# Six weight staging buffers and earlier loads of layer 1's vectors in a two-layer hybrid diffusion kernel

## The chip, the cores and the metric

The kernel runs on one core of one Trainium2 chip. The metric is the device time of one execution in microseconds (us), given as the median of several runs. Lower is better.

## What is computed

Two layers act on 256 latent tokens `x` and 256 context tokens, each of width 1024. Each layer modulates a normed input with vectors made from `c` (for the latent) and `c_ctx` (for the context), projects it once, and feeds three mixers: latent attention over all keys (MLA), windowed attention with sinks (SWA), and a gated delta rule in chunks of 64, run in both directions. Their outputs are gated, summed and projected; a gated MLP with a depthwise convolution follows.

```python
for l in range(DEPTH):                       # DEPTH = 2
    m_lat = modulation(c, w_mod[l], b_mod[l])        # silu(c) @ w_mod + b_mod, split in 6
    m_ctx = modulation(c_ctx, w_mod[l], b_mod[l])
    xn = adaln(x, norm1[l], m_lat[0], m_lat[1])
    hn = adaln(h, norm1[l], m_ctx[0], m_ctx[1])
    y_lat, y_ctx = token_mixer(xn, hn, ...)          # MLA + SWA + gated delta, merge, w_out
    x = x + m_lat[2] * y_lat
    x = x + m_lat[5] * conv_ffn(adaln(x, norm2[l], m_lat[3], m_lat[4]), ffn_up[l], ffn_conv[l], ffn_down[l])
    ...                                              # h likewise, except in the last layer
return rmsnorm(x, norm_f)
```

All tensors are float32. The kernel keeps that precision by splitting each operand in a rounded high part and a low rest and multiplying three times.

## The kernel before

All tokens lie side by side, 512 columns, features on the partitions. A weight piece of 512 KB (four blocks of 128 input rows by 256 output columns) goes through `load_split` (L181 to L190): SyncE (SP) starts its DMA into a buffer of tag `raw`, ScalarE (ACT) casts it to `wh` (L189), VectorE (DVE) makes the rest `wl` (L179, called from L190), and TensorE (PE) multiplies each block three times in `mm3` (L199 to L201). There are `nr` = 3 buffers `raw`, `nh` = 3 of `wh` and `nl` = 4 of `wl`. A `raw` buffer is free again when its `wl` has been made.

The modulation vectors need 1024 x 6144 weights per layer. For layer 0, `mod_part` (L583 to L605) loads them in pieces of 128 x 1024 into the same `raw` buffers (L591), without casting them, and PE multiplies each piece as it stands (L593). Two generators of this work, `mods[0]` and `mods[1]`, fill gaps of layer 0: the first the scan of the delta rule (`gdn_scan`, from L923), the second the attentions. A `raw` buffer of theirs is free when PE has multiplied it.

The small vectors of a layer (biases, norms, the rows of a convolution) are loaded as rows of one tile by `load_vectors` (L538 to L559): nine DMAs, then two transposes on PE (L558) and two copies on DVE (L559). `load_conv` (L561 to L572) does the same for the 132 rows of an MLP convolution: two DMAs (128 rows at L567, 4 rows at L568), two transposes (L570, L571) and one copy. Layer 0's vectors load through GpSimd (POOL) at the start; layer 1's vectors and both convolutions load through SP at the start of layer 0's attentions (L1465 to L1468), all into buffers of tag `b2`, of which there are seven.

The order on each engine comes from a list scheduler of the framework: it takes instructions by priority as their inputs become ready in its own model. Each engine then works strictly in that order, and so does SP with its DMAs: a load whose buffer isn't free holds up every load behind it. DMAs on SP also wait for earlier ones, because their completion semaphores are reused in turn.

```python
        raw = self.sb(shape, "raw", F32, self.NRAW)
        for view, src in srcs:
            nc.sync.dma_start(out=view(raw), in_=src)
        H = self.sb(shape, "wh", F32R, self.NWH)
        L = self.sb(shape, "wl", F32R, self.NWL)
        nc.scalar.copy(H, raw)
        self.split_L(L, raw, H)
```

Of the kernel before, what the change touches and what calls it, by code (L numbers as in the profile page):

```python
# [5 lines left out]
F32 = mybir.dt.float32  # L6
# [12 lines left out]
DEPTH = 2  # L19
# [10 lines left out]
def make_consts():  # L30
# [58 lines left out]
    l1={}, s2=(2, 1, 2, 0), pe=(0.0, 0.1, 0.0, 0.0), ov=0, np=(0.1, 0.0, 0.25, 0), ly=2, qs=(0, 4), dec1=3.0, dec2=4.0, sol1=4.2, sol2=4.0,  # L89
    sol3=1.0, sol4=2.0, sca=(1.0, 2.0), scb=(1.0, 2.0), scc=(1.0, 2.0),   cap=12.0, sl=(0.3, 0.3, 0.5, 0.1), modc=(4.0, 0.9),  # L90
    lag=(0, 0, 2, 4, 5), nmod=(2, 5), hk=(5, 12), f0=(1.0, 1.6, 1.0, 1.0, 1.5, 1.0, 1.0), f1=(1.0, 1.0, 1.0, 0.3, 1.0, 1.0, 0.3), lat=1.0,
    bx=4, wd=0, dc=1, gk=(0, 0), hpe=60, w_t=5, w_k=3, w_s=0, w_r=1.5, w_n=3, w_o=4.0, nr=3, nh=3, nl=4, nb2=7, st=0, ab=(0.0, 0.0, 0.0, 0.0),
    st2=6, bge=2, hpa=40, hpn=0, hpk=40, hpv=40)

_INS = ["x", "c", "ctx", "c_ctx", "w_mod", "b_mod", "norm1", "norm2", "w_in", "mla_q_norm", "mla_kv_norm",
# [5 lines left out]
NVEC = 114  # L101
# [33 lines left out]
class Kernel:  # L135
# [402 lines left out]
    def load_vectors(self, l):  # L538

        nc, i = self.nc, self.ins  # L540
        q = nc.gpsimd if l == 0 else nc.sync
        ident = self.con("ident")
        rows = self.b2([128, 128])
        for nm, (r0, n) in VEC_ROWS.items():
            if nm == "gdn_norm":
                for h in range(2):
                    q.dma_start(out=rows[r0:r0 + 1, h * 64:h * 64 + 64], in_=i[nm][l:l + 1, :])
                continue
            a = i[nm] if nm == "norm_f" else i[nm][l]
            if nm == "gdn_conv":  # L550
                a = a.rearrange("t (r c) -> (t r) c", c=128)
            else:
                a = a.rearrange("(r c) -> r c", c=128)
            q.dma_start(out=rows[r0:r0 + n, :], in_=a)
        for a, b in ((0, 56), (56, NVEC)):
            yield
            ps = self.ps([128, T], "g")
            nc.tensor.transpose(ps[:, :b], rows[:b, :], ident[:b, :b])  # L558
            nc.vector.tensor_copy(self.vec[l][:, a:b], ps[:, a:b])  # L559

    def load_conv(self, l):  # L561

        nc, i = self.nc, self.ins
        ident = self.con("ident")
        fr = i["ffn_conv"][l].rearrange("t (r c) -> (t r) c", c=128)
        f0, f1 = self.b2([128, 128]), self.b2([128, 128])
        nc.sync.dma_start(out=f0, in_=fr[0:128, :])  # L567
        nc.sync.dma_start(out=f1[:4, :], in_=fr[128:132, :])  # L568
        ps = self.ps([128, T], "g")
        nc.tensor.transpose(ps[:, :128], f0, ident)  # L570
        nc.tensor.transpose(ps[:, 128:132], f1[:4, :], ident[:4, :4])  # L571
        nc.vector.tensor_copy(self.fcv[l], ps[:, :132])  # L572

    def v(self, l, nm):
        o, n = VEC_ROWS[nm]
# [721 lines left out]
    def layer(self, l):  # L1297
        nc, i = self.nc, self.ins
# [5 lines left out]
        n = self.qw = S if last else T  # L1304
# [77 lines left out]
        def push(*gens):  # L1382
            self.gsync()
            at = self.queue.index(self.gates) if self.gates in self.queue else len(self.queue)
            self.queue[at:at] = gens
# [5 lines left out]
        def chain(*gens, f=1.0, burst=0.0):  # L1391

            gens, value = list(gens), None
            while gens:
                for g in list(gens):
                    try:
                        self.fill(f * next(g), burst)
                    except StopIteration as e:
                        gens.remove(g)
                        value = e.value  # L1400
            return value
# [15 lines left out]
        spill = self.dram.tile([128, KD, T], F32, name=f"spill{l}")  # L1417
        for j in range(2):
            nc.sync.dma_start(out=spill[:, j * 4:j * 4 + 4], in_=self.xT[j])
        self.mark(f"gtab_{l}")  # L1420
        chain(self.gdn_tables(l), f=P[f"f{l}"][5])
        self.mark(f"gdec_{l}_0")
# [33 lines left out]
        if last:  # L1456
            t = self.s8([128, 8, n])
# [3 lines left out]
        nh = 8 // len(qh)  # L1461
        snk = self.sm([128, 8])
        nc.sync.dma_start(out=snk, in_=i["swa_sink"][l].partition_broadcast(128))
        if l == 0:
            for _ in self.load_vectors(1):  # L1465
                pass
            for j in range(DEPTH):
                self.load_conv(j)  # L1468
        push(*([gsp, mods[1]] if l == 0 else [gsp]))
        self.modcost = self.P["modc"][1]  # L1470
        ga = self.attend(streams, lambda h: ((qh[h // nh][:, h % nh, :], kh[h // 4][:, h % 4, :]),),
# [47 lines left out]
        for bi, ((gi, b), y) in enumerate(zip(gate_br, (yc, ya, yb))):  # L1519
# [4 lines left out]
            for u in range(4):  # L1524
                gate_load(bi * 4 + u + 2)
                if bi * 4 + u in ahead:
                    t = ahead.pop(bi * 4 + u)
# [61 lines left out]
        for half in range(2):  # L1589
            aH, aL = [], []  # L1590
            for a in (aH, aL):
                for al, m_ in ((self.s8, 4), (self.s8, 4), (self.b4, 2), (self.b4, 1)):
                    t = al([128, m_, T], F32R)
                    a += [t[:, k] for k in range(m_)]
            f0 = half * 11
# [124 lines left out]
```

## Time and profile before

| | before |
|---|---|
| median of 3 runs | 1764.64 us (1761.48 to 1771.3) |
| profiled execution | 1760.08 us, its span 1758.3 us |
| busy in the span: PE, DVE, ACT, POOL | 1668.4, 1160.7, 777.4, 217.0 us |
| mean granted TensorE clock | 0.976 of full speed |
| DMA traffic | 228.75 MB, mean 130 GB/s |

The busy time is a sum over stages with different limits; a stretch in which PE is idle is read with the engine and line that ended the idle time. The span is the profiled stretch; 1.8 us of the execution lie outside it.

### The profile page before, as it was taken

How to read it: one execution, taken by the hardware profiler on the slowest of the kernel's cores; microseconds unless marked ns; L12 is line 12 of the kernel's file. 1: busy time of each engine (PE TensorE's matmuls, PEld its weight loads, DVE VectorE, ACT ScalarE, POOL GpSimd, SP SyncE). 2: the span in 40 equal slices, each digit the busy share in tenths (PEclk: the TensorE clock that was granted, in tenths of full speed). 3: DMA queues.
4: the chain of work that ended last, by engine and by line, in shares of the span. 5: the costliest groups of instructions: out<-in, count | busy, mean ns of one | idle time of the engine just before them, and what ended most of it. 6: DMA issues, size and time to landing. Idle time of an engine off the chain costs nothing. (4 is left out here: it accounts for less than half of the span.)

```text
span 1758.3 us, 31525 instructions
## 1 busy us (share of the span) xinstructions
PE 1668.4 (95%) x12723; PEld 1355.3 (77%) x12723; DVE 1160.7 (66%) x2223; ACT 777.4 (44%) x1377; POOL 217.0 (12%) x217
## 2 busy tenths in 40 slices
PE   6989998998999999999999999989988899999997
PEld 3768766775557888668888888778887667999997
DVE  3888697675775534545435553699997877667684
ACT  3664412234665233324324433465532575556463
POOL 1000000002100312011001111020302301212010
PEclk9999998998999999999999999999897999999999
DMA  9424335333135533853233343434351223745663
GB/s 348 118 59 122 103 100 172 74 87 101 55 102 175 185 124 105 313 186 101 87 105 96 96 157 109 126 90 132 103 130 38 61 85 107 235 145 178 185 186 123
DMA packets 216944, 228.75 MB, mean 130 GB/s; under 512 B 51228, under 2 KB 195422, under 8 KB 215646
## 3 DMA queue, kind: packets, MB, share of 16 engines
q1 hardware_dynamic: 211582, 220.11, 40.9%
q10 hardware_dynamic: 4928, 6.56, 1.0%
q8 instruction: 100, 1.64, 0.4%
q14 instruction: 46, 0.38, 0.1%
q0 software_dynamic: 288, 0.06, 0.0%
HBM read 213.85 MB, written 11.80 MB: 128 GB/s over the span
## 5 line engine op out<-in xcount | busy, mean ns | idle before, releaser
L179 DVE TENSOR_TENSOR wl<-raw,wh 128x1024 fp32r<-128x1024 f32 (+2 forms) x294 | 357.7, 1217 | 236.9 <-ACT wh L189 235.7
L189 ACT CAST wh<-raw 128x1024 fp32r<-128x1024 f32 (+2 forms) x294 | 298.6, 1018 | 382.3 <-PE mm L200 187.6
L199 PE MATMUL mm<-xnh,wh 128*128 128x512 f32 (+2 forms) x1072 | 378.6, 354 | 4.6 <-DVE s L131 1.9
L201 PE MATMUL mm<-xnh,wl 128*128 128x512 f32 (+2 forms) x1072 | 373.2, 351 | 5.0 <-DVE wl L179 4.9
L200 PE MATMUL mm<-xnl,wh 128*128 128x512 f32 (+2 forms) x1072 | 374.4, 350 | 0.0
L199 PEld LDWEIGHTS mm<-xnh,wh 128*128 128x128 f32 (+1 forms) x1072 | 204.8, 191 | 39.2 <-issue 7.7
L201 PEld LDWEIGHTS mm<-xnh,wl 128*128 128x128 f32 (+1 forms) x1072 | 204.3, 191 | 35.6 <-DVE wl L179 7.0
L200 PEld LDWEIGHTS mm<-xnl,wh 128*128 128x128 f32 (+1 forms) x1072 | 204.8, 191 | 27.6 <-issue 4.0
L199 PE MATMUL g<-xnh,wh 128*128 128x256 f32 (+1 forms) x496 | 167.6, 340 | 1.4 <-ACT xnh L405 1.4
L200 PE MATMUL g<-xnl,wh 128*128 128x256 f32 (+1 forms) x496 | 166.3, 337 | 0.2 <-DVE xnl L406 0.2
L201 PE MATMUL g<-xnh,wl 128*128 128x256 f32 (+1 forms) x496 | 166.3, 337 | 0.0
L199 PE MATMUL mm<-s,wh 128*128 128x256 f32 (+1 forms) x458 | 149.4, 328 | 0.7 <-DVE s L534 0.6
L201 PE MATMUL mm<-s,wl 128*128 128x256 f32 (+1 forms) x458 | 149.3, 327 | 0.6 <-DVE wl L179 0.6
L200 PE MATMUL mm<-s,wh 128*128 128x256 f32 (+1 forms) x458 | 149.1, 326 | 0.1
L1620 POOL TENSOR_TENSOR b<-b,b 128x512 f32<-128x512 f32 (+1 forms) x44 | 54.4, 1237 | 442.1 <-DVE b L1604 381.1
L199 PEld LDWEIGHTS g<-xnh,wh 128*128 128x128 f32 x496 | 94.7, 192 | 15.0 <-issue 3.3
L201 PEld LDWEIGHTS g<-xnh,wl 128*128 128x128 f32 x496 | 94.7, 191 | 10.5 <-issue 1.2
L199 PE MATMUL g<-s,wh 128*128 128x512 f32 (+1 forms) x304 | 102.7, 338 | 0.0
L200 PEld LDWEIGHTS g<-xnl,wh 128*128 128x128 f32 x496 | 94.7, 191 | 10.1 <-DVE xnl L406 0.8
L200 PE MATMUL g<-s,wh 128*128 128x512 f32 (+1 forms) x304 | 102.2, 336 | 0.0
L201 PE MATMUL g<-s,wl 128*128 128x512 f32 (+1 forms) x304 | 102.1, 336 | 0.0
L199 PEld LDWEIGHTS mm<-s,wh 128*128 128x128 f32 x458 | 86.8, 190 | 8.8 <-DVE s L534 1.1
(290 smaller groups left out, 2699.0 us busy)
## 6 DMA issues: line engine op xcount, KB each, us to landing
raw<-in_w_in_dram SPq DMA_DIRECT2D x92, 512.0 KB
raw<-in_ffn_up_dram SPq DMA_DIRECT2D x80, 512.0 KB
s<-in_w_mod_dram SPq DMA_DIRECT2D x64, 512.0 KB
raw<-in_w_mod_dram SPq DMA_DIRECT2D x32, 512.0 KB
raw<-in_ffn_down_dram SPq DMA_DIRECT2D x32, 512.0 KB
raw<-in_w_out_dram SPq DMA_DIRECT2D x16, 512.0 KB
raw<-in_ffn_down_dram SPq DMA_DIRECT2D x16, 384.0 KB
spill<-s SPq DMA_DIRECT2D x4, 1024.0 KB
```

The lines of the kernel that those rows point to most:

```text
L179: self.nc.vector.tensor_tensor(out=out, in0=x, in1=h.bitcast(F32), op=ALU.subtract)
L189: nc.scalar.copy(H, raw)
L199: mm(ps, lhsT=wH, rhs=xH, start=start, stop=False)
L200: mm(ps, lhsT=wH, rhs=xL, start=False, stop=False)
L201: mm(ps, lhsT=wL, rhs=xH, start=False, stop=stop)
L1620: nc.gpsimd.tensor_tensor(out=y[:, cs], in0=y[:, cs], in1=av[t][:, cs], op=ALU.mult)
```

## The change

Six buffers `raw` stand in place of three; the room for them comes from a smaller scratch area for the descriptors that POOL writes for its own DMAs (2048 bytes in place of the default). `load_vectors(1)` and `load_conv` are split at a `yield`: their DMAs are issued right after layer 0's spill of the residual stream, ahead of the delta rule's tables, into three buffers of a new tag `rows`; transposes and copies stay at the start of layer 0's attentions. The four last rows of each convolution go into the vectors' tile, and the second transpose of each convolution takes that whole tile (122 rows). Each convolution is copied in two pieces.

```diff
-    bx=4, wd=0, dc=1, ... w_o=4.0, nr=3, nh=3, nl=4, nb2=7, ...
+    bx=4, wd=0, dc=1, ... w_o=4.0, nr=6, nh=3, nl=4, nb2=7, ...
@@ load_vectors
-        rows = self.b2([128, 128])
+        rows = self.b2([128, 128]) if l == 0 else self.sb([128, 128], "rows", F32, 3)
+        if l:
+            self.rows = rows
+            for j in range(DEPTH):
+                q.dma_start(out=rows[NVEC + 4 * j:NVEC + 4 * j + 4, :], in_=i["ffn_conv"][j].rearrange("t (r c) -> (t r) c", c=128)[128:132, :])
@@ load_conv
-        f0, f1 = self.b2([128, 128]), self.b2([128, 128])
+        f0, n = self.sb([128, 128], "rows", F32, 3), NVEC + 4 * DEPTH
         nc.sync.dma_start(out=f0, in_=fr[0:128, :])
-        nc.sync.dma_start(out=f1[:4, :], in_=fr[128:132, :])
+        yield
         ps = self.ps([128, T], "g")
         nc.tensor.transpose(ps[:, :128], f0, ident)
-        nc.tensor.transpose(ps[:, 128:132], f1[:4, :], ident[:4, :4])
-        nc.vector.tensor_copy(self.fcv[l], ps[:, :132])
+        nc.tensor.transpose(ps[:, 128:128 + n], self.rows[:n, :], ident[:n, :n])
+        nc.vector.tensor_copy(self.fcv[l][:, :128], ps[:, :128])
+        nc.vector.tensor_copy(self.fcv[l][:, 128:132], ps[:, 128 + NVEC + 4 * l:132 + NVEC + 4 * l])
@@ layer, after the spill
+        if l == 0:
+            small = [self.load_vectors(1)] + [self.load_conv(j) for j in range(DEPTH)]
+            for g in small:
+                next(g)
@@ layer, at the start of the attentions
         if l == 0:
-            for _ in self.load_vectors(1):
-                pass
-            for j in range(DEPTH):
-                self.load_conv(j)
+            for g in small:
+                for _ in g:
+                    pass
@@ kernel
-    nc = bacc.Bacc("TRN2", target_bir_lowering=False, num_devices=1)
+    nc = bacc.Bacc("TRN2", target_bir_lowering=False, num_devices=1, dynamic_dma_scratch_size=2048)
```

Three places show how the instructions move. Lines in the changed file are 4 to 9 higher from the edits on: L554 becomes L558, L558 becomes L562, L591 and L593 become L596 and L598, L1051 becomes L1056, L1233 becomes L1238, L1419 becomes L1424.

SP, the loads queued ahead of layer 0's attentions, before (`raw` from `in_w_mod` are the pieces of `mods[1]`; `b_599`, `b_602`, `b_603` hold the vectors and convolution rows):

```order
L591 DMA raw_4487<-in_w_mod_dram 128x1024
L591 DMA raw_4493<-in_w_mod_dram 128x1024
L1463 DMA sm_4092<-in_swa_sink_dram 128x8
L591 DMA raw_4559<-in_w_mod_dram 128x1024
L591 DMA raw_4565<-in_w_mod_dram 128x1024
L554 DMA b_599_4094<-in_b_mod_dram 48x128
...
L567 DMA b_602_4110<-in_ffn_conv_dram 128x128
L568 DMA b_603_4111<-in_ffn_conv_dram 4x128
...
L591 DMA raw_4617<-in_w_mod_dram 128x1024
L591 DMA raw_4623<-in_w_mod_dram 128x1024
```

and in the change:

```order
L596 DMA raw_4487<-in_w_mod_dram 128x1024
L596 DMA raw_4493<-in_w_mod_dram 128x1024
L596 DMA raw_4559<-in_w_mod_dram 128x1024
L596 DMA raw_4565<-in_w_mod_dram 128x1024
L596 DMA raw_4617<-in_w_mod_dram 128x1024
L1472 DMA sm_4108<-in_swa_sink_dram 128x8
L596 DMA raw_4623<-in_w_mod_dram 128x1024
L596 DMA raw_4689<-in_w_mod_dram 128x1024
```

The thirteen small loads are gone from this place, and the modulation pieces follow each other.

PE at the same place, before (`g_4051` is the rotary product of MLA's queries, `mm_4486` the modulation, `g_4104` to `g_4122` the transposes, `g_4126` and `g_4135` the first scores of the attention):

```order
L593 MATMUL mm_4486<-raw_4487,cT 32x256 x4
L593 MATMUL mm_4486<-raw_4493,cT 32x256
L1233 MATMUL g_4077<-b_593_4075,cst 128x256
L593 MATMUL mm_4486<-raw_4493,cT 32x256 x3
L593 MATMUL mm_4486<-raw_4559,cT 32x256 x4
L593 MATMUL mm_4486<-raw_4565,cT 32x256 x4
L558 MATMUL g_4104<-cst,b_599_4094 128x56
L558 MATMUL g_4107<-cst,b_599_4094 128x114
L570 MATMUL g_4114<-cst,b_602_4110 128x128
L571 MATMUL g_4114<-cst,b_603_4111 128x4
L570 MATMUL g_4122<-cst,b_605_4118 128x128
L1051 MATMUL g_4126<-s_490_3462,s_572_3968 128x256
```

and in the change:

```order
L598 MATMUL mm_4486<-raw_4493,cT 32x256
L1238 MATMUL g_4093<-b_596_4091,cst 128x256
L562 MATMUL g_4110<-cst,rows_652 128x56
L562 MATMUL g_4113<-cst,rows_652 128x114
L574 MATMUL g_4116<-cst,rows_664 128x128
L575 MATMUL g_4116<-cst,rows_652 128x122
L574 MATMUL g_4121<-cst,rows_666 128x128
L575 MATMUL g_4121<-cst,rows_652 128x122
L1056 MATMUL g_4126<-s_493_3478,s_575_3984 128x256
L1056 MATMUL g_4135<-s_493_3478,s_575_3984 128x256
L598 MATMUL mm_4486<-raw_4493,cT 32x256 x3
L598 MATMUL mm_4486<-raw_4559,cT 32x256 x4
```

The transposes and the first two scores now stand ahead of eleven modulation products that they stood behind.

SP at the start of layer 0's delta stage, before (`spill` is the residual stream on its way to memory, `raw_669` the first weights of the next projection):

```order
L186 DMA raw_626<-in_w_in_dram 128x4x32 x2
L1419 DMA spill_649<-s_9_104 128x2048
L1419 DMA spill_649<-s_10_105 128x2048
L186 DMA raw_669<-in_w_in_dram 128x4x256
L186 DMA raw_756<-in_w_in_dram 128x4x256
```

and in the change:

```order
L1424 DMA spill_649<-s_10_105 128x2048
L547 DMA rows_652<-in_ffn_conv_dram 4x128 x2
L558 DMA rows_652<-in_b_mod_dram 48x128
L558 DMA rows_652<-in_norm_dram 8x128 x2
...
L571 DMA rows_664<-in_ffn_conv_dram 128x128
L571 DMA rows_666<-in_ffn_conv_dram 128x128
L186 DMA raw_685<-in_w_in_dram 128x4x256
L186 DMA raw_772<-in_w_in_dram 128x4x256
```

The thirteen loads now stand between the spill and the first weights of the projection.

## Rows read from the trace of the kernel before

**Rows 1.** The page: span, and busy time (share of the span) of each engine.

```profile
span 1758.3 us, 31525 instructions
PE 1668.4 (95%) x12723; PEld 1355.3 (77%) x12723; DVE 1160.7 (66%) x2223; ACT 777.4 (44%) x1377; POOL 217.0 (12%) x217
```

**Rows 2.** Stretches: length, busy us (instructions) of each engine, granted clock, DMA share, GB/s.

```profile
240.00:285.00 45.00, 37.94 (x623) 25.53 (x622) 39.10 (x99) 5.99 (x12) 0.00 (x0) 0.92 0.58 188
268.00:271.40 3.40, 3.40 (x56) 2.47 (x54) 2.21 (x2) 1.11 (x4) 0.00 (x0) 0.51 0.77 270
417.00:425.00 8.00, 8.00 (x32) 4.40 (x32) 4.44 (x16) 4.28 (x11) 0.93 (x1) 0.50 0.62 217
530.00:1100.00 570.00, 568.14 (x2912) 458.35 (x2912) 272.93 (x384) 203.16 (x295) 74.48 (x61) 1.00 0.44 142
1100.00:1500.00 400.00, 366.05 (x3682) 302.79 (x3681) 330.86 (x701) 200.51 (x383) 68.03 (x71) 0.95 0.36 97
```

**Rows 3.** Waits of PE, whole span: us in total, times, longest.

```profile
PE mm L593 <- DMA raw<-in_w_mod_dram: 6.6, 6, 2.8
PE mm L201 <- DVE wl L179: 5.6, 5, 3.5
```

**Rows 4.** Timeline of PE, 407 to 425: start, us, operation [idle before, releaser].

```profile
408.53 0.70 PE L1233 MATMUL g<-b,cst 128*128 128x256 f32 x2
409.16 1.06 PE L593 MATMUL mm<-raw,cT 128*32 128x256 f32 x14
413.04 0.64 PE L593 MATMUL mm<-raw,cT 128*32 128x256 f32 x8 [2.82 <-DMA raw<-in_w_mod_dram]
...
414.95 0.42 PE L558 MATMUL g<-cst,b 114*128 114x114 f32 x1 [1.07 <-DMA b<-in_gdn_norm_dram]
...
416.79 1.06 PE L1051 MATMUL g<-s,s 96*128 96x256 f32 x2
...
424.39 0.69 PE L1098 MATMUL g<-cst,b 128*128 128x128 f32 x2
```

**Rows 5.** Timeline of SP's queue, 395 to 424.

```profile
395.86 12.72 SPq L591 DMA_DIRECT2D raw<-in_w_mod_dram  x2
408.62 0.44 SPq L554 DMA_DIRECT2D b<-in_b_mod_dram  x1
...
411.07 2.17 SPq L547 DMA_DIRECT2D b<-in_gdn_norm_dram  x2
...
415.54 8.47 SPq L591 DMA_DIRECT2D raw<-in_w_mod_dram  x5
```

**Rows 6.** Timeline of DVE, 396 to 425.

```profile
409.80 1.71 DVE L1242 TENSOR_TENSOR s<-b,b 32x256 f32<-32x256 f32 x4
...
417.89 0.42 DVE L131 TENSOR_REDUCE sm<-g 128x1 f32<-128x256 f32 x1 [1.38 <-PE g L1051]
```

**Rows 7.** Waits of PE, 225 to 310 (layer 0's first scan).

```profile
PE mm L593 <- DMA raw<-in_w_mod_dram: 3.2, 4, 1.2
```

**Rows 8.** Waits of SP's queue, 225 to 310.

```profile
SPq L591 <- PE mm L593: 23.6, 10, 15.5
```

**Rows 9.** Timelines of SP's queue from 36 and 225, and of ACT from 40 and 275.

```profile
39.90 1.24 SPq L1419 DMA_DIRECT2D spill<-s  x2
44.42 12.98 SPq L186 DMA_DIRECT2D raw<-in_w_in_dram  x3
...
57.61 1.04 ACT L189 CAST wh<-raw 128x1024 fp32r<-128x1024 f32 x1
...
276.71 7.27 SPq L186 DMA_DIRECT2D raw<-in_w_in_dram  x4
...
281.27 1.04 ACT L189 CAST wh<-raw 128x1024 fp32r<-128x1024 f32 x1 [5.73 <-DMA raw<-in_w_in_dram]
```

**Rows 10.** POOL's own loads: its queue, one issue (median us to landing), timelines of POOL and PE.

```profile
q0 software_dynamic: 288, 0.06, 0.0%
...
b<-in_norm_dram POOLq DMA_DIRECT2D x2, 4.0 KB, 5.4
...
1.26 0.77 POOL L554 DMA_DIRECT2D b<-in_b_mod_dram  x1 [0.83 <-POOLq L1708]
...
45.28 0.26 PE L558 MATMUL g<-cst,b 114*128 114x114 f32 x1
```

More of the change, by code (lines that the diff above doesn't have):

```diff
@@ L91 @@
     lag=(0, 0, 2, 4, 5), nmod=(2, 5), hk=(5, 12), f0=(1.0, 1.6, 1.0, 1.0, 1.5, 1.0, 1.0), f1=(1.0, 1.0, 1.0, 0.3, 1.0, 1.0, 0.3), lat=1.0,
-    bx=4, wd=0, dc=1, gk=(0, 0), hpe=60, w_t=5, w_k=3, w_s=0, w_r=1.5, w_n=3, w_o=4.0, nr=3, nh=3, nl=4, nb2=7, st=0, ab=(0.0, 0.0, 0.0, 0.0),
+    bx=4, wd=0, dc=1, gk=(0, 0), hpe=60, w_t=5, w_k=3, w_s=0, w_r=1.5, w_n=3, w_o=4.0, nr=6, nh=3, nl=4, nb2=7, st=0, ab=(0.0, 0.0, 0.0, 0.0),
     st2=6, bge=2, hpa=40, hpn=0, hpk=40, hpv=40)
```

## The prediction

> **What bounds the kernel.** The page comes first. PE is busy 95% of the span and no other engine passes 66% [rows 1], so time can come only from PE's idle time, about 90 us, and from stretches in which the clock is low. The stretches then say where these lie [rows 2]. From 530 to 1100 PE is busy 568.1 of 570 us at full clock: three buffers already hide the loads there. From 1100 to 1500 (layer 1's mixers) PE is idle 34 us, but DVE is busy 331 of 400 us there. The waits of PE, sorted by what ended them, say which of the idle time is a load's [rows 3]: 6.6 us in six waits are modulation products waiting for a `raw` piece, and 5.6 us in five waits are third products waiting for `wl`. No wait of a weight product on a `raw` load is among PE's: such pieces pass through a cast and a split, and there DVE was late, not the load.
>
> Four of the six waits lie in layer 0's first scan, 3.2 us together [rows 7]. One, of 2.82 us, stands at the start of layer 0's attentions, with a wait of 1.07 us for the small vectors right behind it [rows 4]. The sixth is the rest, 0.6 us.
>
> **Term 1, the start of layer 0's attentions.** PE ends the last rotary product at 409.2 (408.53 + 0.70), works through modulation products, waits, transposes the vectors, waits again, and starts the first scores at 416.79 [rows 4]. SP shows why: the modulation pieces stand one behind the other for buffers until 408.62, and the thirteen small loads fill the queue until the next piece is issued at 415.54 [rows 5]. In the change the small loads have landed some 360 us before, six pieces are queued ahead instead of four, and PE's order has the six transposes right behind the rotary product, then two scores, and only then the eleven modulation products. Six transposes at 0.42 us [rows 4] are 2.5 us, so the first score starts near 411.7, 5.1 us earlier. DVE is free for it: its last rotary sums start at 409.80 and take 1.71 us, and it has waited until 417.89 for the first score to reduce [rows 6]. The two added DVE copies lie in that idle time and cost nothing; were it gone, they would cost as much as two small copies.
>
> How much of it lasts to the first transposed probabilities (L1098 at 424.39)? Between the first score and there PE is never idle but runs at a granted clock of 0.50, the lower level of 1.2 GHz [rows 2], behind the two waits, 3.9 us together. The eleven products (22 records, 1.06 + 0.64 = 1.7 us at full clock [rows 4]) now come inside. If the clock stays low, the work from first score to L1098 takes 7.6 + 3.4 us and L1098 comes at 422.7: a gain of 1.7 us. If it stays high, 3.8 + 1.7 us, and L1098 comes at 417.2: a gain of 7.2 us. I take 6.0, near the upper end: the two waits ahead of the low stretch go, but DVE's chain from scores to probabilities, 4.4 us busy in these 8 [rows 2], will not halve. The rest of the attentions follows from these first units, so it moves with them.
>
> **Term 2, the first scan.** SP waits 23.6 us for PE to free modulation buffers, once for 15.5 us [rows 8]; then PE uses sixteen pieces faster than they come. With six buffers three more pieces lie ready, and the waits of 3.2 us go. Right behind them the clock is 0.51 for 3.4 us with PE busy throughout [rows 2]; at the full 2.4 GHz that work takes 1.7 us less. Upper end 4.9 us. The lower end is nothing: DVE is busy 39.1 of 45 us here [rows 2], and PE's next scan products wait for DVE anyway. I take half, 2.4.
>
> **Term 3.** The sixth wait, 0.6 us, goes.
>
> **What moves to where it may cost.** The thirteen issues took 6.9 us (408.62 to 415.54 [rows 5]) and now stand behind the spill, which SP issues at 39.90 and 1.24 us long. The first weights behind them are then issued near 48.1 instead of 44.42. They are cast at 57.61; a load on that queue took 4.6 us from issue to cast (276.71 to 281.27), so any issue before 53.0 is in time [rows 9]. This cover is 4.9 us. Further on, the order of DVE and PE differs in a few places: a `wl` of the gates is made some twenty instructions later in the first decay, and a few products change places in layer 1. I price that at nothing, between 2 us lost and 2 us gained, as the 5.6 us that PE waits for `wl` in five places [rows 3] can shift by one such place of a little over 1 us each.
>
> **The sum.** 6.0 + 2.4 + 0.6 = 9.0 us. Against the profiled execution, 1760.08 us, that is 1751.1. The median of the three runs is 4.6 us above that execution; against it the forecast is 1764.64 - 9.0 = 1755.6 us. The ends: 1.7 + 0 + 0.6 - 2 = 0.3 us gained, and 7.2 + 4.9 + 0.6 + 2 = 14.7 us. A measurement of this kernel can tell about 0.5%, 8.8 us, from no change.
>
> **Rivals.** *The chains take the place of the loads.* In the scan DVE, and in the attentions the chain PE, DVE, ACT, PE, end the waits next, and the clock stays low where these begin. For it: PE also waits for DVE in the scan, and only 6.6 us of PE's 90 are named as this change's. Against it: DVE stood idle ahead of the first score. It gives 0 to 4 us, about 1762.5.
>
> *The clock comes back everywhere.* Every low stretch near these two places goes, and the products that wait on ACT in the attentions find more time. It gives the upper end, 13 to 16 us: about 1750.
>
> *SP's queue holds up the first layer.* The thirteen loads stand behind a spill of 2 MB. One pair of them took 2.17 us in the old place, as the second had to wait for an earlier load to land [rows 5]. If each of the thirteen waits like this at the new place, at 2.0 us each, they end at 67 (41.1 + 26); the weights are 14 us later than the 53.0 at which they have to be issued, and DVE, which works behind them on the first decay, has no idle time to make it good. It decides at a delay of 4.9 us beyond mine, and each further us is one of the whole layer. Price 14, less a gain of 9.0: 1769.6, and 1778 if the first rival is true as well. For it: loads of this queue do wait for one another. Against it: most of the thirteen took 0.25 to 0.5 us.
>
> *POOL's loads queue up.* The scratch area for its descriptors is smaller. Its nine loads (288 packets) are issued one behind the other from 1.26, and land after about 5.4 us [rows 10]. If each had to wait for the one before it, the last would land at 1.26 + 9 x 5.4 = 49.9, and the second transpose of layer 0's vectors, at 45.28, would be 4.6 us late: 1760.2 with the gain. No row shows how large the area must be. The Trainium skill (Debugging Trainium Hangs, section "4. Descriptor Overflow") speaks against the change here: too many descriptors for this area on POOL's queue are a cause of hangs. Its page DMA: Bandwidth & Descriptors ("Terms") gives a descriptor 16 bytes, from which I estimate 128 per ring in 2048 bytes; 288 packets over sixteen engines are 18 each, so by these pages the area suffices, and nothing here shows how near the limit lies.
>
> That the change doesn't do what it says is part of the first rival: the order of SP shows six modulation pieces in a row, so the buffers are used.
>
> **Chances.** The forecast, with gains from 4 to 13 us, has 0.60; the chains 0.19; the clock 0.08; SP's queue 0.09; POOL's loads 0.04. Of the forecast's 0.60, two thirds (0.40) lie beyond 8.8 us; with the clock's 0.08 that is 0.48 for faster. The rest of it, the chains, POOL's loads and 0.01 of SP's queue are 0.44; slower by over 0.5% has 0.08. The range goes from the upper end of the gains, 1750, to no gain, widened by 0.5 us on the fast side and 1 us on the slow: 1749.5 to 1765.6. It leaves out SP's queue and the outer part of the clock's case.
>
> **What would show it.** In the changed profile the waits of PE for `raw` modulation pieces should be under 1 us in all, the first scores should follow the last rotary product by about 2.5 us with the transposes between them, and the granted clock from there to the first probabilities should be near 1. SP should issue the thirteen loads between about 36 and 48, and the first cast behind them should wait for PE or ACT, not for its load. In the first scan PE's idle time should fall from 7.1 us in 45 towards 4. If instead PE's waits for loads are gone and the waits for DVE in the same stretches have grown by as much, the first rival holds. A PE waiting for `wl` or casts between 57 and 80 would make the forecast wrong from SP's side, and a second transpose of layer 0's vectors that starts after 46 from POOL's.

## Result and profile after

| | before | after |
|---|---|---|
| median of nine runs each, us | 1770.09 | 1753.40 |
| lowest run, us | 1761.48 | 1748.95 |
| profiled execution: time, span, granted clock | 1760.08, 1758.3, 0.976 | 1754.3, 1752.5, 0.973 |

One of before's nine runs took 4045.81 us and, as a slow one, does not count in the ratio on record, 0.9932, with a 95% interval of 0.9914 to 0.9950: 12 us less, between 9 and 15. The medians in the table lie further apart, 16.7 us; in thirty more runs before's median was 1764.40 (1758.70 to 1771.83), 11.0 above the change's. The forecast was 9.0 us less, 1755.6 us, with a range of 1749.5 to 1765.6.

The two profiled executions are only 5.8 us apart, as that of before lies some 4 us below before's median. So a single pair of profiles says where time went, and the medians say how much. The page's rows that answer to [rows 1]:

```profile
span 1752.5 us, 31516 instructions
PE 1662.9 (95%) x12723; PEld 1358.3 (78%) x12723; DVE 1160.4 (66%) x2225; ACT 782.8 (45%) x1379; POOL 209.3 (12%) x217
```

PE has 5.5 us less busy time for the same 12723 products, though its mean clock is no higher (0.973 to 0.976); 4.7 us less are found at the start of the attentions, where the clock stayed up (below). Its idle time, span less busy, is the same as a whole: 89.9 and 89.6 us. What went in one place came back in others. PE's waits over the whole span, against [rows 3]:

```profile
PE g L960 <- DVE b L949: 12.0, 9, 4.9
PE g L1103 <- DVE sm L131: 6.4, 4, 3.1
PE mm L201 <- DVE wl L179: 6.0, 5, 2.4
```

The row of [rows 3] on modulation products that wait for `raw` is gone altogether (in a second profile of the change, r1 below, 1.5 us in two waits are left, both in the first scan). At the top stands a wait for DVE. In the first scan the waits that answer to [rows 7] are these, all of them:

```profile
PE g L960 <- DVE b L949: 5.0, 4, 2.7
PE g L974 <- DVE b L964: 1.6, 2, 0.8
PE g L911 <- issue: 1.4, 1, 1.4
PE g L989 <- DVE b L983: 0.6, 1, 0.6
```

The timeline of PE at the start of layer 0's attentions, against [rows 4]:

```profile
408.74 0.70 PE L1238 MATMUL g<-b,cst 128*128 128x256 f32 x2
409.37 0.51 PE L562 MATMUL g<-cst,rows 56*128 56x56 f32 x2
...
410.05 0.27 PE L575 MATMUL g<-cst,rows 122*128 122x122 f32 x1
410.16 1.03 PE L1056 MATMUL g<-s,s 96*128 96x256 f32 x4
411.12 1.93 PE L598 MATMUL mm<-raw,cT 128*32 128x256 f32 x32
...
416.50 0.44 PE L1103 MATMUL g<-cst,b 128*128 128x128 f32 x2
```

No wait stands between the last rotary product and the first score, which comes 1.42 us behind the former's start instead of 8.26. The timeline of SP's queue, against [rows 5, 9]:

```profile
39.13 3.23 SPq L1424 DMA_DIRECT2D spill<-s  x2
42.42 1.98 SPq L547 DMA_DIRECT2D rows<-in_ffn_conv_dram  x2
...
50.38 0.83 SPq L571 DMA_DIRECT2D rows<-in_ffn_conv_dram  x2
51.30 8.53 SPq L186 DMA_DIRECT2D raw<-in_w_in_dram  x6
...
391.28 0.42 SPq L1472 DMA_DIRECT2D sm<-in_swa_sink_dram  x1
396.07 21.11 SPq L596 DMA_DIRECT2D raw<-in_w_mod_dram  x9
```

The weights behind the thirteen loads are issued at 51.30, in place of 44.42, and at the attentions nine modulation pieces follow each other where [rows 5] has the small loads. Stretches: first those of [rows 2], and then three that begin and end at the same products in both kernels (first scan; start of the attentions; the step from the first attention to the second):

```profile
240.00:285.00 45.00, 38.33 (x623) 28.29 (x619) 42.12 (x105) 7.17 (x13) 0.00 (x0) 0.93 0.60 200
...
530.00:1100.00 570.00, 566.01 (x2912) 459.83 (x2911) 274.52 (x383) 202.03 (x290) 75.25 (x62) 1.00 0.45 145
1100.00:1500.00 400.00, 363.81 (x3684) 302.71 (x3683) 328.20 (x693) 201.91 (x384) 67.82 (x70) 0.95 0.35 96
...
247.60:333.20 85.60, 77.48 (x1327) 58.68 (x1327) 62.21 (x135) 18.18 (x30) 2.30 (x3) 0.94 0.50 146
406.00:434.10 28.10, 27.24 (x183) 16.91 (x182) 24.62 (x81) 20.31 (x59) 12.15 (x16) 1.00 0.43 151
460.70:499.80 39.10, 35.94 (x205) 22.14 (x204) 22.77 (x76) 20.70 (x62) 0.00 (x0) 0.83 0.47 148
```

The same three of before:

```profile
243.60:332.00 88.40, 79.85 (x1328) 58.09 (x1328) 62.64 (x136) 18.18 (x30) 2.30 (x3) 0.94 0.47 141
405.80:442.20 36.40, 31.97 (x176) 18.98 (x176) 25.13 (x78) 20.17 (x59) 12.10 (x16) 0.86 0.33 108
470.60:506.20 35.60, 32.07 (x207) 19.48 (x205) 22.77 (x78) 20.84 (x62) 0.00 (x0) 0.95 0.45 148
```

The scan is 2.8 us shorter, but PE's idle time in it only 0.4 (8.1 in place of 8.5), at the same clock of 0.94. The start of the attentions is 8.3 us shorter: PE idles 0.9 us in place of 4.4, and its granted clock is 1.00 in place of 0.86. The step is 3.5 us longer, with a clock of 0.83 in place of 0.95: here part of the gain is given back.

### The profile page after: what moved, and what is told of

It is laid out like the page before. It is cut to its first block, busy times and chain, and to the rows that moved or that the text cites. A ratio compares the mean times of both kernels' runs of the same rounds, so it can differ in the third digit from the quotient of the medians.

```text
span 1752.5 us, 31516 instructions
## 1 busy us (share of the span) xinstructions
PE 1662.9 (95%) x12723; PEld 1358.3 (78%) x12723; DVE 1160.4 (66%) x2225; ACT 782.8 (45%) x1379; POOL 209.3 (12%) x217
## 5 line engine op out<-in xcount | busy, mean ns | idle before, releaser
L1628 POOL TENSOR_TENSOR b<-b,b 128x512 f32<-128x512 f32 (+1 forms) x44 | 46.3, 1052 | 447.8 <-DVE b L1612 405.5
```

Of the source, the lines that this page charges most:

```text
L1628: nc.gpsimd.tensor_tensor(out=y[:, cs], in0=y[:, cs], in1=av[t][:, cs], op=ALU.mult)
```

## Experiments

Three measures are used. The ratio to before, from runs on the same chip. The profile, product by product: the n-th product of a line and a result is paired with that of before, and the table at the end gives by how much each stretch grew or shrank. And the time at the lower clock: each run lists its span and mean granted clock, and span x (1 - clock) / 0.5 is the time at the lower level; half of it is what the low level cost if PE was busy throughout (it counts too much where PE waited). Time and clock are listed for every run; a profile is of one execution.

**e1: six buffers alone.** Before with `nr=6` and the small scratch area; the small loads stay.

```diff
-    ... w_o=4.0, nr=3, nh=3, ...
+    ... w_o=4.0, nr=6, nh=3, ...
...
-    nc = bacc.Bacc("TRN2", target_bir_lowering=False, num_devices=1)
+    nc = bacc.Bacc("TRN2", target_bir_lowering=False, num_devices=1, dynamic_dma_scratch_size=2048)
```

> Six raw buffers and the small scratch area, with the thirteen small loads left where they were. Theory (the start of the attentions is worth some 8 us by the early loads, the scan some 3 us by the buffers, and the thirteen loads cost the first layer some 4 us): PE's waits for modulation pieces in the first scan go (3.2 us to under 1), those at the start of the attentions stay near 2.8 us, the first layer up to 250 us stays as before, and the time is 3 us below before, between 1 and 5. Rival (the six buffers alone also let the pieces queue past the small loads, so they carry most of the gain): 8 us or more below before. Rival (nothing of the scan's gain lasts): within 1 us of before.

Median 1761.07, ratio 0.9986 (0.9971 to 1.0002): 2.5 us less, from 5 less to nothing, so not told apart from no change by this run alone. The waits in the scan fall from 3.2 us to 0.3. At the start of the attentions the pieces still stand behind the small loads, as its timeline of PE shows:

```profile
408.67 0.64 PE L593 MATMUL mm<-raw,cT 128*32 128x256 f32 x8 [2.04 <-DMA raw<-in_w_mod_dram]
...
410.64 0.42 PE L558 MATMUL g<-cst,b 114*128 114x114 f32 x1 [1.14 <-DMA b<-in_ffn_conv_dram]
...
418.62 0.66 PE L1098 MATMUL g<-cst,b 128*128 128x128 f32 x2
```

**e2 and its repeat r2: early loads alone.** The change with `nr=3`.

> The change with three raw buffers in place of six; the early loads stay. Theory: the scan keeps its 3.2 us of waits, the start of the attentions loses its wait for the small vectors and has the transposes ahead of the modulation products, the first score comes 5 to 7 us earlier than before, and the first layer is as late as in the change (3 to 4 us by 104 us). Net 2 to 6 us below before, and 3 to 6 above the change. Rival (the buffers carry the gain): no faster than before, since the first layer is later and the pieces still wait for buffers. Rival (the first layer's delay is not from the loads): 8 us or more below before.

Median 1756.92, ratio 0.9952 (0.9930 to 0.9974). The repeat, beside the change:

> The change with three raw buffers, again. Theory: the early loads carry the gain; the time is within 3 us of the change. Rival (the buffers are worth what the scan shows and nothing is given back): 3 us or more above the change.

Median 1757.63, ratio 0.9958 (0.9935 to 0.9981). So the early loads alone bring 7.4 to 8.5 us, more than the 2 to 6 that were expected, and the scan keeps its waits (4.0 us in five). The first layer runs as in before up to 250 us in e2 (-0.2 us, against the 3 to 4 late that were expected) and is 1.6 us late in r2, by the same instructions: what the change's own profile lost there is for the larger part the execution's. In time at the lower clock, before had a mean of 100 us in thirty runs, e2 86 and r2 90, but six buffers alone 107: the two halves pull the clock in opposite directions.

**r1: the change again.**

> The change itself, beside the next three on one chip. Theory (six buffers gain some 3.3 us in layer 0's first scan and lose some 3.6 us at 476 to 506, where the modulation products run out early, and some 2.7 us in layer 1's second solve, where a split stands ahead of the stream transposition on DVE): the time is 9 to 13 us below before and within 3 us of the change with three buffers. The stretches at 50 to 250 us, 2.4 to 4 us later than before in the one profile, are within 1.5 us of before here, if that delay was the execution's and not the change's; rival: 3 to 4 us later again.

Median 1753.92, ratio 0.9939 (0.9919 to 0.9959). The two halves add up: 2.5 and 7.4 to 8.5 us, against 10.8 here and 12 at first. The repeats, on one chip, put the change 3.7 us ahead of early loads alone by their medians (1753.92 to 1757.63), 3.8 by their means, with a 95% interval of 0.9 to 6.7 worked out from the twelve runs of each: the buffers do add something (r2's theory had allowed 3 us).

**e3: the small scratch area alone.** Before, with the second line of e1's diff.

> The kernel before with the small scratch area alone. Theory: POOL's loads land as before, the second transposition of layer 0's vectors stays near 45.3 us, and the time is within 1 us of before. Rival (POOL's loads queue up): the second transposition comes after 49 us and the time is 4 us or more above before.

Median 1764.33, ratio 0.9998 (0.9983 to 1.0013). The second transposition starts at 46.07, the whole stretch around it being 0.8 us late. In the change it starts at 47.72, with everything there 2.4 us late. The Trainium skill (Debugging Trainium Hangs, section "4. Descriptor Overflow") names too many descriptors for this area as a cause of hangs on POOL's queue. Here 288 packets pass through 2048 bytes without a trace of it.

**e4: the thirteen loads later.** The change, with the issue of the small loads moved from behind the spill to the start of the first scan.

```diff
         if l == 0:
             small = [self.load_vectors(1)] + [self.load_conv(j) for j in range(DEPTH)]
-            for g in small:
-                next(g)
         self.mark(f"gtab_{l}")
...
         alloc_zsq()
+        if l == 0:
+            for g in small:
+                next(g)
```

> The change with the thirteen small loads issued when the first scan begins, about 210 us later than in the change and still some 170 us before they are needed. Theory (the loads behind the spill delay the first layer by 4 us): the first layer up to 250 us runs as before, the gains in the scan and the attentions stay, and the time is 3 to 4 us below the change. Rival (the first layer's delay in the one profile comes from the clock at the start, 23 to 33 us, or from the order of the products there): within 1.5 us of the change. Rival (the loads now stand between the modulation pieces at the scan): the scan's waits come back and the time is 2 us or more above the change.

Median 1754.98, ratio 0.9937 (0.9915 to 0.9960): the same as the change. The stretch from 57 to 244 us is as long as in before; over the nine profiles with the thirteen loads issued early it is 0.5 us longer on average (from 0.4 shorter to 1.5 longer), over the three without (e1, e3, e4) 0.4 shorter. One wait marks the difference. In the change, between 57 and 80 us, it is PE's only one:

```profile
PE mm L201 <- DVE wl L179: 2.4, 1, 2.4
```

It stands, 2.4 us long, in each of those nine profiles, and in neither before nor e1, e3 and e4. So the place of the thirteen loads costs a wait of 2.4 us, of which about 1 us lasts.

**e8: thirteen loads made thirty-nine.** The change, with 26 loads more behind them.

```diff
             for g in small:
                 next(g)
+            fr = i["ffn_conv"][0].rearrange("t (r c) -> (t r) c", c=128)
+            t = self.sb([128, 128], "rowx", F32, 1)
+            for j in range(26):
+                nc.sync.dma_start(out=t[4 * j:4 * j + 4, :], in_=fr[4 * j:4 * j + 4, :])
```

> The change with 26 more loads of 4 rows behind the thirteen, into a tile that nobody reads. Theory (the first weights behind the loads are in time while they are issued before 53.0; in the change they were issued at 51.3): at 0.53 us an issue, as the thirteen took 6.9 us, the 26 take 13.8 us more, the weights are issued near 65, 12 us too late, PE then waits for wl or casts between 57 and 80, and the run is 8 to 13 us above the change. Rival (DVE's tables and decay set the pace of this stretch, and the weights have more room than I worked out): under 3 us above the change.

Median 1764.16, ratio 0.9987 (0.9966 to 1.0008), some 9 us above the change by the ratios. Its timeline of SP's queue:

```profile
50.26 9.31 SPq L1432 DMA_DIRECT2D rowx<-in_ffn_conv_dram  x26
59.61 2.77 SPq L732 DMA_DIRECT2D sm<-in_gdn_dt_bias_dram  x4
62.43 2.51 SPq L732 DMA_DIRECT2D sm<-in_gdn_a_log_dram  x4
65.04 4.04 SPq L186 DMA_DIRECT2D raw<-in_w_in_dram  x6
```

The 26 take 9.3 us, and eight loads of the decay, which the change has behind the first weights, now come ahead of them. The weights go out 13.7 us later than in the change, and the stretch from 57 to 244 us is 9.1 us longer than in before, 7.6 and 8.2 longer than in the change's two profiles: some 0.6 us for each us of delay. PE's waits from 50 to 110 us are not for `wl` or casts, as was expected:

```profile
PE g L720 <- DVE s L716: 7.6, 2, 4.6
PE g L776 <- ACT gtb L753: 4.4, 1, 4.4
```

They are for the norms of the keys (L716) and the tables of the decay (L753). In the change, products of these weights fill PE from 65.8 us on, ahead of these two and between them; here the first of them starts at 84.91, behind both, and ACT casts the first weights at 80.94, though they were issued at 65.04. So the delay acts at least in part through the order, which the scheduler makes by its own model, and a low stretch of 13.7 us from 73.9 on, amid these waits (3.4 in the change), is part of the price. The forecast's rival, that SP's queue holds up the first layer, is real, but cheaper than its 1 us for each us; how much is the queue's and how much the order's is not shown. The change issues the weights 1.7 us ahead of the point (53.0) from which it was to decide.

**e6: three buffers for weights, three for modulation pieces.** The change with `nr=3` and a tag of its own for the pieces.

```diff
-            t = ... self.sb([128, D], "raw", F32, self.NRAW)
+            t = ... self.sb([128, D], "rawm", F32, 3)
```

> The change with six buffers as three for weights and three for the modulation's pieces. Theory (the third split ahead of the stream transposition in layer 1 comes from a fourth weight buffer): the split is behind the transposition again, layer 1's second solve loses nothing against before (between 1300 and 1330 us, under 0.5 us; the change lost 2.9), and the scan's waits stay mostly away (under 1.5 us of 3.2). 1 to 3 us below the change. Rival (the delay in layer 1 has another cause, such as the clock): the same 2.5 us are lost there.

Median 1759.70, ratio 0.9961 (0.9936 to 0.9985): if anything slower than the change, a miss in its sum. In layer 1's second solve nothing is lost (0.0 us from 1300 to 1329; e1, e4, e8 and both profiles of the change lost 2.9 each). But the step between the attentions cost 4.1 us, the start of the attentions gained 5.5 and not 8, and the scan gained nothing: PE waits 6.4 us for pieces there (under 1.5 was expected), and its stretch is about 2 us longer than in before.

**e7: three more buffers for the scan alone.** As e6, but only every second piece of the first scan's modulation takes the second tag.

> The change with three raw buffers and three more that only every second modulation piece of layer 0's first scan uses. Theory: it keeps the scan's gain (3 us), the early loads' gain (8 us), and neither the idle time behind 476 us nor the loss in layer 1's second solve; 3 to 6 us below the change and 14 to 17 below before. Rival (the gain in the scan is lost again by 500 us whatever the buffers do): the same time as the change with three buffers.

Median 1753.52, ratio 0.9938 (0.9913 to 0.9963): no better than the change. The scan's 3.3 us are there and layer 1 loses nothing, but the start of the attentions gains 5.2 us and not 8, and 6.8 us go between 471 and 506, with PE's order that of e2 in both places, which gained 8.1 and lost none. PE's waits in that stretch:

```profile
PE g L1103 <- DVE sm L131: 2.6, 1, 2.6
PE mm L598 <- DMA raw<-in_w_mod_dram: 1.7, 1, 1.7
```

Behind the 1.7 us the granted clock is at the lower level for 20.5 us. In e2 the same wait for a piece lasted 0.4 us, and the only low stretch there, behind the wait for DVE, 3.4. At the start of the attentions, too, e7 has a wait of 1.7 us for a piece and a low stretch of 6.8 us, and e2 a wait of 1.2 and none.

**e9: six buffers in layer 0, three in layer 1.** Loads of layer 0 take turns between two tags of three; layer 1 uses one.

```diff
+    def rawtag(self):
+        self.turn = not getattr(self, "turn", False)
+        return "rawm" if self.turn and self.lay == 0 else "raw"
...
-        raw = self.sb(shape, "raw", F32, self.NRAW)
+        raw = self.sb(shape, self.rawtag(), F32, 3)
...
-            t = ... self.sb([128, D], "raw", F32, self.NRAW)
+            t = ... self.sb([128, D], self.rawtag(), F32, 3)
```

> The change with six buffers in layer 0 and three in layer 1 (loads of layer 0 take turns between two sets of three; layer 1 uses one set). Theory: layer 0 runs as in the change, up to 550 us; in layer 1's second solve the split stands behind the stream transposition, and the 2.7 to 2.9 us that the change lost between 1316 and 1329 in both of its profiles are not lost. 2 to 3 us below the change, 13 to 14 below before. Rival (what is not lost there is lost later in layer 1, or in another low-clock stretch): the same as the change.

Median 1752.05, ratio 0.9924 (0.9898 to 0.9951): 1.9 us below r1, but with overlapping intervals, so the gain over the change shows in the profiles and not in the times. The mechanism in layer 1 is shown by DVE's timelines. In the change:

```profile
1304.65 1.19 DVE L179 TENSOR_TENSOR wl<-raw,wh 128x1024 fp32r<-128x1024 f32 x1
...
1306.16 1.22 DVE L179 TENSOR_TENSOR wl<-raw,wh 128x1024 fp32r<-128x1024 f32 x1
...
1307.68 1.22 DVE L179 TENSOR_TENSOR wl<-raw,wh 128x1024 fp32r<-128x1024 f32 x1
...
1309.05 3.75 DVE L131 STREAM_TRANSPOSE s<-s 128x1024 f32<-128x1024 f32 x2
...
1325.02 0.42 DVE L949 TENSOR_TENSOR b<-s,b 128x256 f32<-128x256 f32 x1
```

and in e9:

```profile
1300.62 1.19 DVE L183 TENSOR_TENSOR wl<-raw,wh 128x1024 fp32r<-128x1024 f32 x1
...
1302.13 1.22 DVE L183 TENSOR_TENSOR wl<-raw,wh 128x1024 fp32r<-128x1024 f32 x1
...
1304.00 3.75 DVE L131 STREAM_TRANSPOSE s<-s 128x1024 f32<-128x1024 f32 x2
...
1310.73 1.95 DVE L183 TENSOR_TENSOR wl<-raw,wh 128x1024 fp32r<-128x1024 f32 x1
...
1314.10 0.75 DVE L953 TENSOR_TENSOR b<-s,b 128x256 f32<-128x256 f32 x2
```

With six buffers the third split has its weights early and is put ahead of the transposition for which PE waits (PE's wait there is 4.9 us in the change, 4.0 in e9 and before). It takes 1.2 us, and the order behind it comes out differently too: the second of the products with `s` (L949, L953) ends 16.4 us behind the transposition's start in the change, 10.9 in e9, and PE waits 4.9 us for it in the change. Three buffers put the split behind the transposition, in before, e2, r2, e3, e6, e7, e10 and here, and none of these lost more than 0.3 us. (e11, with three buffers in layer 1 and the split behind, lost 2.7 there; its orders differ in all of layer 1.)

**e10: transposes in the scan.** e9, with the transposes and copies of the small vectors at the end of the first scan.

```diff
         finish(gkv)
+        if l == 0:
+            for g in small:
+                for _ in g:
+                    pass
```

> The kernel of the run before this one, with the transposes and copies of the small vectors moved from the start of the attentions to the end of layer 0's first scan. Theory (the start of the attentions gained because the first score follows the last rotary product; the six transposes still stand between them, 2.5 us): the first score follows within 1 us, and the scan, where DVE is the bound and PE idles 6 us of 45, pays under 2 us for them; 0.5 to 2.5 us below the run before this one. Rival (the transposes cost the scan what they give back): within 0.5 us. Rival (the start of the attentions waits for DVE instead): within 0.5 us, with a wait of PE for DVE where the transposes stood.

Median 1749.53, ratio 0.9915 (0.9886 to 0.9944): the lowest of all, 15 us below before, though its interval overlaps the change's and, with six runs each, e9's. The first score follows the rotary product, and PE then waits a little for DVE:

```profile
402.97 0.70 PE L1242 MATMUL g<-b,cst 128*128 128x256 f32 x2
403.50 2.32 PE L1060 MATMUL g<-s,s 96*128 96x256 f32 x10
...
409.37 0.41 PE L1107 MATMUL g<-cst,b 128*128 128x128 f32 x2 [0.82 <-DVE b L1097]
```

The start of the attentions is 1.2 us shorter than in e9, and the scan pays nothing for the transposes.

**e11: the products spread over the attentions.** e9, with the cost at which the kernel's planner books a modulation step in layer 0's attentions at 1.4 in place of 0.9.

```diff
-        self.modcost = self.P["modc"][1]
+        self.modcost = self.P["modc"][1] if l else 1.4
```

> The kernel of e9 with the cost by which the planner spreads layer 0's modulation products over the attentions at 1.4 in place of 0.9. Theory (the products run out near 475 us, PE then waits 3 us for DVE and its clock is at the lower level for 13.7 us): the products last 10 to 20 us longer, the low stretch behind 476 us shrinks to 3.4 us or goes, and the time is 2 to 5 us below e9. Rival (the wait at the step from one attention to the next has nothing to do with the products): the wait and the low stretch stay, at 470 to 500 us, and the time is within 1 us of e9, or above it since the products now come with the second attention's units, where DVE is busier.

Median 1762.74, ratio 0.9979 (0.9959 to 0.9999): a miss. The products last until 481 (472 in e9), PE still waits 2.1 us for DVE behind them (3.0 in e9), the low stretch is 20.5 us long and not shorter, and the orders of layer 1 change as well, for a loss of some 8 us between 1144 and the end. The clock tells more: over all runs the mean time at the lower level is 119 us, against 96 in e9, and half the difference is about the whole loss of 10 us. The wait at the step from one attention to the next has moved with the end of the products: its longest part stands at the 117th record of its line (L1107 here), where e9 and the change have it at the 101st, and before, whose products last longer than theirs, at the 109th. So stretching the products shifts the wait and does not remove it. What sets the length of the low stretch behind it stays open: it was 3.4 us in the four profiles with three buffers (before, e2, r2, e3), and 10.2 to 20.5 us in all ten with more in layer 0.

The stretches of the profiled executions, us more or less than before's:

| from to (us in before) | change | r1 | e1 six alone | e2 early alone | r2 | e9 | e10 |
|---|---|---|---|---|---|---|---|
| start to 57 | +2.4 | +0.7 | +0.9 | -0.2 | +0.3 | +0.2 | -1.1 |
| 57 to 244 | +1.5 | +0.9 | -0.7 | 0.0 | +1.3 | -0.2 | +1.0 |
| 244 to 332, first scan | -2.7 | -3.0 | -4.1 | +0.4 | +2.6 | -2.1 | -4.3 |
| 332 to 406 | -1.0 | -1.0 | -1.1 | 0.0 | 0.0 | -1.1 | -1.1 |
| 406 to 442, start of attentions | -8.4 | -8.6 | +0.8 | -8.1 | -8.2 | -8.6 | -9.8 |
| 442 to 471 | -1.8 | +1.0 | -1.8 | -1.4 | -1.4 | -1.8 | -1.6 |
| 471 to 506, step to the second attention | +3.6 | +4.4 | +3.6 | -0.2 | -0.1 | +3.6 | +3.6 |
| 506 to 1300 | +0.6 | +0.9 | -2.0 | -0.6 | -0.8 | +0.2 | +0.3 |
| 1300 to 1329, layer 1's second solve | +2.9 | +2.9 | +2.9 | 0.0 | +0.1 | 0.0 | 0.0 |
| 1329 to the end | -3.0 | -3.0 | +2.5 | +3.4 | +4.5 | -0.1 | -0.1 |

The last row differs between executions: low stretches of 3.4 and 6.8 us come and go there without any difference of this change that was found. One question no run puts by itself: the early loads also bring a new order of PE at the start of the attentions, and the two were not tried apart.

## Why the prediction was right, step by step

- **What bounds the kernel.** Right for the place of the main gain, the start of the attentions: PE's idle time, and the low clock beside it. That the loads of the rest were hidden holds too: from 530 to 1100 PE is busy 566.0 of 570 us, as before.
- **Term 1, start of the attentions, 6.0 us (1.7 to 7.2).** The mechanism is right, the size too small: 7.9 us to the first transposed probabilities (424.39 to 416.50), more than the upper end, and 8.1 to 8.6 us to 442 in the five profiles of the table with early loads and the transposes still there (5.5 and 5.2 in e6 and e7). Two steps were mis-sized. The six transposes took 0.8 us and not 2.5: the 0.42 us in [rows 4] was that of one at the lower clock behind a wait, and back to back they start 0.11 us apart. And the clock stayed at the upper level throughout. Against this, 54 records of modulation products, and not 40, came between the first score and these probabilities. That it is the early loads, not the buffers, is shown by e1 (+0.8) and e2 (-8.1).
- **Term 2, first scan, 2.4 us (0 to 4.9).** 2.7 and 3.0 us in the change's two profiles, and nothing with three buffers. The size came out, and not by the path: the 3.2 us of waits for pieces went, but 2.9 of them came back as waits for DVE (L960 from 3.5 to 5.0 us, L974 from 0.2 to 1.6), which is the first rival's sign. PE's idle time between 240 and 285 went only from 7.1 to 6.7 us, where I had named 4, and over the whole scan from 8.5 to 8.1, with the same 10.2 us at the lower clock. What became shorter is PE's busy time, and of that 2.1 us the modulation products' own (128 records, 11.1 to 9.0 us), a term that the sum does not have. Why they took longer with three buffers stays open.
- **Term 3, 0.6 us.** The sixth wait stood at 486, in the step between the attentions. It went with the others, but that stretch grew by 3.5 us.
- **Terms 2 and 3 together, 3.0 us**, are close to what six buffers alone gave, 2.5 us with an interval that reaches nothing, but for another reason than the sum said. Their 3 to 5 us up to 406 are partly given back in two places that the forecast did not name: at the step between the attentions (3.6 us, low clock) and in layer 1's second solve (2.9 us, order on DVE).
- **Order shifts, nothing (2 lost to 2 gained).** Here the forecast failed in kind: one shift cost 2.9 us in every profile with six buffers in layer 1. I had looked for late splits; this one is early, on the engine that sets the pace.
- **Thirteen loads, hidden.** Held in the main, not wholly. They took 8.9 us (42.42 to 51.30) and not 6.9, so the weights went out at 51.30 and not 48.1, still ahead of 53.0. But the casts of 1024 columns begin at 63.58 and not near the 57.61 of before, without idle time of ACT ahead of them, behind other work of ACT's new order, and PE waits 2.4 us for `wl` between 57 and 80: the very sign that I had named against the forecast from SP's side. It cost about 1 us. The deadline was worked out from an order that the change did not keep. e8 shows the price beyond, some 0.6 us for each us.
- **The number** came closer than its parts. In the pair of profiles the two places of terms 1 and 2 gained 11.1 us, 2 more than the whole sum, and the rest of the kernel lost 5.3; that losses which nobody had forecast made up in part for a term put too low is luck.
- **Rivals.** The chains (1762.5) are true of the scan, by their sign almost wholly; the clock (1750) is true of the start of the attentions and the contrary behind 471; SP's queue is real but not reached; POOL's loads fell with e3. The second transposition at 47.72, past the 46 that I had named as POOL's sign, was the whole stretch being late: by 32 us, ahead of it, the change is 2.4 us behind, with a low stretch of 10.2 us from 22.7 in place of 3.4. The 1778 for two rivals at once does not follow from their parts: 1762.5 and 14 make 1776.5.

## What to carry to other kernels

A load that stands in a queue between others delays what is queued behind it: moving thirteen small loads to a place with room was worth 8 us, twice what their waits show, as the clock of TensorE stayed up behind them. The price of a late load, too, came by way of the order: in e8 the scheduler had put other work first. More buffers are not free even where there is room: an operation that gets its data earlier may be put earlier, ahead of one for which the bound engine waits, so look at the order of the busiest engine wherever the buffers are shared, and give the extra ones only to the stage that lacks them (e9's profile shows the gain of this; its time is not told apart from the change's). Compare a part of a change by itself in enough runs: executions of one kernel differ here by more than the parts.

## What the runs showed of the hardware

The low stretch behind a wait of PE has no fixed length, and the wait doesn't set it. At the step between the attentions it was 3.4 us behind a wait of 2.9 us in before, 13.7 behind 3.1 in the change, and 20.5 in e6, where it began at 480.8 us and PE's only wait, of 0.9 us, at 480.9, with PE busy almost throughout. In e7 it was 20.5 us with the order of PE that had 3.4 in e2. In e11 it was 20.5 us too, and its stretches were

```profile
480.00:490.00 10.00, 7.63 (x38) 4.06 (x37) 9.29 (x29) 8.20 (x23) 0.00 (x0) 0.87 0.91 300
490.00:500.00 10.00, 10.00 (x29) 5.11 (x28) 5.19 (x17) 4.71 (x15) 0.00 (x0) 0.50 0.15 51
500.00:510.00 10.00, 10.00 (x36) 6.11 (x36) 4.93 (x17) 4.39 (x12) 0.00 (x0) 0.60 0.01 2
```

0.50 is the lower of the two levels, 1.2 GHz. If the time at the lower level is taken out (span less half of it), executions of one kernel agree better: the standard deviation falls from 3.4 to 2.8 us in the thirty runs of before (mean 1713.1) and from 3.9 to 0.9 in the nine of the change. By this measure six buffers alone are 6.5 us faster than before and early loads alone 1.8; the clock then takes 3.8 us from the former and gives 6.8 to the latter.
